# Small products of an RWKV-7 recurrence spread over four array positions instead of two, in a one-core decoder step

## The chip, the cores and the metric

The kernel runs on one core of a Trainium2 chip. A core has a matrix engine (TensorE, "PE" in the profile, its weight loads "PEld"), VectorE ("DVE"), ScalarE ("ACT"), GpSimd ("POOL") and SyncE, whose queue ("SPq") issues the transfers. The metric is the device time of one execution in microseconds (us), median of several runs; lower is better. For a shorter look at one execution there is a profile, with a trace of every instruction.

## The reference

One layer of a decoder trunk on 256 prompt rows and 8 x 4 sample rows, width 2048. A combined input projection feeds two groups of heads, a retention group (8 heads of 256) and an RWKV-7 group (32 heads of 64); one output projection closes the layer. The change lies in the RWKV group:

```
def rwkv7_recurrence(r, w, k, v, kk, a, s0):
    def step(s, inp):
        r_t, w_t, k_t, v_t, kk_t, a_t = inp
        sa = jnp.einsum('bhvk,bhk->bhv', s, -kk_t)
        s = (s * w_t[:, :, None, :] + sa[..., None] * (kk_t * a_t)[:, :, None, :]
             + v_t[..., None] * k_t[:, :, None, :])
        return s, jnp.einsum('bhvk,bhk->bhv', s, r_t)
...
o_rw = group_norm(o_rw, RWKV_GN_EPS) * ln_x_w + ln_x_b
o_rw = o_rw + jnp.sum(r_h * k_h * r_k, axis=-1, keepdims=True) * v_h
y = (jnp.concatenate([y_ret, y_rw], axis=-1) @ w_out)
```

## The kernel before

**Projections.** The inputs `h` and the weights are split into a high and a low fp32r part; each block of weights is loaded (`raw`), split (`whi` by ScalarE, `wlo` by VectorE or GpSimd) and multiplied three times into `acc` (high x high, high x low, low x high). These 128x288 products are most of TensorE's work and the filler between everything else.

**Head pairs.** The RWKV heads are worked in eight rounds q = 0 to 7 of four heads (`rwkv_blocks(q)`); within a round p = 0, 1 are the two tile halves and h (or x) the two heads on partitions 0 to 63 and 64 to 127. The 256 prompt rows are 8 chunks of 32 (`CH`); the sample rows are a ninth "chunk" (c = 8). A tile row of 64 holds two kinds of rows of 32: in `SC` (the masked products), `UV` and `XR` the lower 32 partitions of each head belong to the unknowns of the recurrence, the upper 32 to values and outputs. `quad(h, i)` is quarter i of head h, 32 partitions.

A round goes: `main_gen` makes `AR` and `BK`, multiplies them into `scp` and masks them into `SC`; `turn_gen` turns `BK` into `BKt`, with half of `UV` as scratch; `inv_gen` inverts the 32x32 triangles by a 15-step recurrence on VectorE and two products (`iva`, `ivb`); `main_gen` turns the values into `UV` and multiplies them (`avp`) into `XR`; `chain_gen` walks the eight chunks, three dependent products each (`ch`: XR by WT, UV by BKt, S by AR); `sample_gen` does c = 8; `out_gen` multiplies `SC` by `UV` (`ops`), adds it to `XR`, normalises, turns it back (`on`) and writes `y`.

**What sets the order.** The program is written by one pass in which every generator yields; `tick` steps those whose modelled inputs are ready by a clock of modelled costs, between groups of three projection products. `wait(name)` and `flag(name)` are dependencies between generators at that time, `drain` steps the generators until a flag is set, with no projection product in between. Tiles with one tag share memory, so that a new one must wait for the old one's readers: `UV`, `AR`, `BK`, `XR` have one buffer each. `AR` of round q has tag AR for even q and BK for odd q; in round 7 `BK` takes tag AR. `pch` has two PSUM buffers ("ch") and `ptp` three.

A product of few rows and columns takes only part of the 128x128 array: its input partitions choose rows, its output partitions choose columns. `mm` and `mm4` issue the same matmul; `mm4` only tells the cost model that consecutive products go to four different positions. All matmuls of this group are fp32, and each appears in the trace as two passes, each with its own weight load.

**The end.** The output projection (`out_group`) needs `y` split into `yhi`, `ylo` in the order of `korder`; its first sixteen k tiles lie in `O[0]` to `O[8]`, and `split_gen` does not start on `O[9]` before round 7's `y` is done (flag `("rw", 7)`). In the list of blocks, `od` (nine blocks) stands ahead of the first block that needs `O[9]`, and is itself behind `drain(("ops", 7))`.

Of the kernel before, what the change touches and what calls it, by code (L numbers as in the profile page):

```python
# [10 lines left out]
F32 = mybir.dt.float32  # L11
F32R = mybir.dt.float32r
AF = mybir.ActivationFunctionType
# [88 lines left out]
def tile_hybrid_step(  # L102
# [585 lines left out]
    def rwkv_blocks(q):  # L688
# [95 lines left out]
        def main_gen():  # L784
# [17 lines left out]
            yield  # L802
            yield from wait(("la", q))
            if q > 1:
                yield from wait(("ops", q - 2))
            ar = mx.tile([P, 2, 9, 2, CH], F32, tag="BK" if q % 2 else "AR", name="AR")
            AR = [ar[:, p] for p in range(2)]
            for p in range(2):
# [35 lines left out]
            UV = mx.tile([P, 2, 9, 64], F32, tag="UV", name="UV")  # L844
            B.update(AR=AR, BKt=BKt, SC=SC, UV=UV)
            mk = K("mwkv")
            flat = lambda t: t.rearrange("p a t -> p (a t)")
            yield PART
# [16 lines left out]
            spawn(bonus_gen(kps))  # L865
            vw = B["vw"]
            yield from wait(("turn", q))
            V.transpose(UV[:, 0, :, 32:64], c9(vw[:, 0, :]))
            yield
            for h in range(2):  # L870
# [81 lines left out]
        def inv_gen():  # L952
# [45 lines left out]
            S.copy(itmp[0:32], ps[0:32, 0:256])  # L998
            V.tensor_copy(itmp[64:96], ps[64:96, 0:256])
            yield PART  # L1000
            ps = tps("ivb")
            for i in range(2 * NC):
                for a in ha2:
                    mm(ps[a.start:a.start + HB, HB * i:HB * i + HB], itmp[a, HB * i:HB * i + HB], wv[a, i, HB:])
            for a in ha2:
                a = slice(a.start, a.start + HB)
                V.tensor_copy(wv[a, :, HB:], ps[a, 0:256].rearrange("s (i t) -> s i t", t=HB))
            yield
            flag(("inv", q))

# [120 lines left out]

        def out_gen():
            SC, UV, XR = B["SC"], B["UV"], B["XR"]
            bst = rwp.tile([P, 18, 6], F32, tag="bst", name="bst")
            gst = rwp.tile([P, 3, 18], F32, tag="gst", name="gst")
            yield PART
            ops, op8 = [pch.tile([P, 512], F32, tag="ch", name="ops") for p in range(2)], tps("ops")
# [8 lines left out]
            tt(V, XR[:, :, 8, :], op8[:, 0:128].rearrange("p (a k) -> p a k", a=2), XR[:, :, 8, :], ADD)  # L1146
            yield from pace(SPC)
            flag(("ops", q))
            for p in range(2):
                for c in range(9):  # L1150
                    V.bn_stats(bst[:, 9 * p + c], XR[:, p, c, :])
# [10 lines left out]
            tt(G, var, var, nhalf[:, 0:18], ALU.pow)  # L1162
            yield
            for p in range(2):
                tt(V, XR[:, p], XR[:, p], gst[:, 0, 9 * p:9 * p + 9].unsqueeze(2).to_broadcast([P, 9, 64]), SUB)
                yield
            for p in range(2):
                o = XR[:, p]
                tt(V, o, o, gst[:, 2, 9 * p:9 * p + 9].unsqueeze(2).to_broadcast([P, 9, 64]), MUL)
# [4 lines left out]
                yield  # L1174
                if p == 1:
                    for h in range(2):
                        S.copy(o[quad(h, 1), :, 0:32], o[quad(1 - h, 1), :, 32:64])
                    yield
                V.transpose(c9(on), o[:, :, 32 - 32 * p:64 - 32 * p])
# [438 lines left out]
```

## Time and profile before

| | |
|---|---|
| median of 3 runs | 1561.44 us (1560.08 to 1562.62) |
| the profiled execution's own time | 1563.12 us |
| its span, first to last instruction | 1561.3 us |
| mean granted TensorE clock | 0.973 of full |
| TensorE / VectorE / ScalarE / GpSimd busy | 94% / 75% / 50% / 30% of the span |

A busy TensorE is one with some matmul in flight. All instructions go through one recording helper, so that the source line is always L255, and a group is known by its tiles: `XR<-ops,XR` writes XR from ops and XR. "32*64 32x64 x72" behind a matmul is the weights' shape (input rows by output rows), what it streams, and how many stand in a row.

### The profile page before, as it was taken

How to read it: one execution, taken by the hardware profiler on the slowest of the kernel's cores; microseconds unless marked ns; L12 is line 12 of the kernel's file. 1: busy time of each engine (PE TensorE's matmuls, PEld its weight loads, DVE VectorE, ACT ScalarE, POOL GpSimd, SP SyncE). 2: the span in 40 equal slices, each digit the busy share in tenths (PEclk: the TensorE clock that was granted, in tenths of full speed). 3: DMA queues.
4: the chain of work that ended last, by engine and by line, in shares of the span. 5: the costliest groups of instructions: out<-in, count | busy, mean ns of one | idle time of the engine just before them, and what ended most of it. 6: DMA issues, size and time to landing. Idle time of an engine off the chain costs nothing. (4 is left out here: it accounts for less than half of the span.)

```text
span 1561.3 us, 37454 instructions
## 1 busy us (share of the span) xinstructions
PE 1463.4 (94%) x14194; PEld 1305.5 (84%) x14194; DVE 1165.6 (75%) x2889; ACT 778.4 (50%) x1698; POOL 462.4 (30%) x469
## 2 busy tenths in 40 slices
PE   4889999999999999899999999999999989999996
PEld 1668887888888878888888899879987977999996
DVE  2434787998788878967987799789878987855453
ACT  2224564464445644644555546545653554455443
POOL 0001322442343145323422353245243422202010
PEclk8889999999999999999999999999999999999998
DMA  9996654674476557645764566466536544675553
GB/s 286 341 347 213 196 156 129 183 195 146 126 240 193 146 146 220 189 119 154 216 182 137 154 180 174 114 170 179 155 101 182 159 133 111 193 237 167 158 162 115
DMA packets 347761, 277.30 MB, mean 178 GB/s; under 512 B 90270, under 2 KB 346110, under 8 KB 346868
## 3 DMA queue, kind: packets, MB, share of 16 engines
q1 hardware_dynamic: 347580, 274.91, 60.5%
q8 instruction: 111, 1.82, 0.5%
q14 instruction: 70, 0.57, 0.1%
HBM read 248.80 MB, written 26.03 MB: 176 GB/s over the span
## 5 line engine op out<-in xcount | busy, mean ns | idle before, releaser
L255 PE MATMUL acc<-Hhi,whi 128*128 128x288 f32 (+2 forms) x2080 | 618.6, 312 | 13.3 <-ACT whi L255 5.3
L255 PE MATMUL acc<-Hlo,whi 128*128 128x288 f32 (+2 forms) x2080 | 618.6, 309 | 0.0
L255 ACT CAST whi<-raw 128x512 fp32r<-128x512 f32 (+1 forms) x648 | 395.4, 618 | 353.0 <-PE acc L255 209.2
L255 POOL TENSOR_TENSOR wlo<-raw,whi 128x512 fp32r<-128x512 f32 x224 | 311.0, 1392 | 758.5 <-ACT whi L255 546.0
L255 PE MATMUL acc<-Hhi,wlo 128*128 128x288 f32 (+2 forms) x2080 | 458.5, 302 | 14.8 <-DVE wlo L255 13.9
L255 PEld LDWEIGHTS acc<-Hhi,whi 128*128 128x128 f32 (+1 forms) x2080 | 397.5, 191 | 42.7 <-issue 11.3
L255 PEld LDWEIGHTS acc<-Hlo,whi 128*128 128x128 f32 (+1 forms) x2080 | 398.4, 192 | 17.3 <-issue 8.1
L255 DVE TENSOR_TENSOR wlo<-raw,whi 128x512 fp32r<-128x512 f32 (+1 forms) x424 | 304.8, 724 | 121.7 <-ACT whi L255 117.0
L255 PEld LDWEIGHTS acc<-Hhi,wlo 128*128 128x128 f32 (+1 forms) x2080 | 340.5, 191 | 22.0 <-DVE wlo L255 19.7
L255 PE MATMUL acc<-ylo,whi 128*128 128x288 f32 x480 | 136.4, 298 | 0.7 <-DVE ylo L255 0.7
L255 PE MATMUL acc<-yhi,whi 128*128 128x288 f32 x480 | 135.9, 298 | 1.0 <-ACT whi L255 1.0
L255 PE MATMUL acc<-yhi,wlo 128*128 128x288 f32 x480 | 101.5, 297 | 0.1
L255 PEld LDWEIGHTS acc<-yhi,whi 128*128 128x128 f32 x480 | 90.4, 188 | 1.4 <-ACT whi L255 1.3
L255 PEld LDWEIGHTS acc<-ylo,whi 128*128 128x128 f32 x480 | 90.4, 188 | 1.3 <-DVE ylo L255 1.0
L255 PEld LDWEIGHTS acc<-yhi,wlo 128*128 128x128 f32 x480 | 76.3, 189 | 0.7 <-POOL wlo L255 0.3
L255 PE MATMUL adaps<-raw,cT 128*32 128x256 f32 x768 | 56.3, 409 | 7.8 <-DMA raw<-in_w_ada_dram 7.8
L255 DVE COPY UV<-ch 32x64 f32<-32x64 f32 x128 | 28.9, 225 | 29.1 <-ACT UV L255 26.1
L255 ACT COPY UV<-ch 32x64 f32<-32x64 f32 x128 | 25.5, 199 | 47.8 <-PE ch L255 46.0
L255 DVE SCALAR_TENSOR_TENSOR s0b<-s0b,ups 128x512 f32<-128x512 f32 x64 | 41.0, 681 | 9.0 <-PE ups L255 8.9
L255 PEld LDWEIGHTS adaps<-raw,cT 128*32 128x32 f32 x768 | 20.2, 114 | 30.4 <-DMA raw<-in_w_ada_dram 15.3
L255 POOL TENSOR_TENSOR rot<-rot,rt 128x288 f32<-128x288 f32 x32 | 29.1, 932 | 44.7 <-DVE rt L255 44.7
L255 DVE SCALAR_TENSOR_TENSOR S<-ch,dec,SP 128x64 f32<-128x64 f32 x112 | 30.5, 278 | 13.8 <-PE ch L255 12.7
(260 smaller groups left out, 1966.8 us busy)
## 6 DMA issues: line engine op xcount, KB each, us to landing
raw<-in_w_in_dram SPq DMA_DIRECT2D x512, 256.0 KB, 3.1
raw<-in_w_ada_dram SPq DMA_DIRECT2D x64, 512.0 KB, 8.3
raw<-in_w_out_dram SPq DMA_DIRECT2D x128, 256.0 KB, 3.0
raw<-in_w_ada_dram SPq DMA_DIRECT2D x64, 256.0 KB, 2.8
s0b<-in_state_ret_dram SPq DMA_DIRECT2D x64, 256.0 KB, 4.6
out_dram<-s0b SPq DMA_DIRECT2D x64, 256.0 KB, 3.2
y<-in_x_prompt_dram SPq DMA_DIRECT2D x4, 1024.0 KB, 6.6
s0r<-in_state_rwkv_dram SPq DMA_DIRECT2D x128, 32.0 KB, 2.8
```

The source lines that it names most:

```text
L255: return f(*a, **k)
```

## The change

It touches the four small products that lie at only two array positions at a time, and what reads them.

`avp` (values): the product for an odd chunk goes to the neighbouring 32 columns, so that four consecutive products lie at four positions; 32 output rows each where there were 64, in one PSUM buffer where there were two. ScalarE then writes it to `XR` with two more copies that move the odd chunks' halves to their place.

`ops` (outputs): only the output columns `CH:` of `SC` are multiplied, 32 output rows each, odd chunks again in neighbouring columns. The sum goes to a tile `O` of its own, five chunk slots for each p where there were nine, laid over `AR`'s memory (over `UV`'s in round 6). Group norm then works on 10 columns and 2 x 320 elements instead of 18 and 2 x 576; sixteen short ScalarE copies in place of six longer ones bring it back into `XR` for the transposes.

`iva`, `ivb` (inversion): the second half's products (p = 1) go to the neighbouring columns; the copies out of PSUM are split in two.

Waits: `AR` of round q waits for `("xr", q - 2)`, which `out_gen` sets after its last transpose, where it waited for `("ops", q - 2)`; in round 7 `turn_gen` waits for `("xr", 6)` before it takes `UV`.

```diff
@@ main_gen
-                yield from wait(("ops", q - 2))
+                yield from wait(("xr", q - 2))
...
-            avps, av8 = [pch.tile([P, 512], F32, tag="ch", name="avp") for p in range(2)], tps("avp")
-            for p in range(2):
-                for c in range(9):
-                    for h in hs2:
-                        v = slice(h.start + 32, h.stop)
-                        t = avps[p][h, 64 * c:64 * c + 64] if c < 8 else av8[h, 64 * p:64 * p + 64]
-                        mm(t, SC[v, p, c, :], UV[v, p, c, :])
-            for p in range(2):
-                act(XR[:, p, 0:8, :].rearrange("p c k -> p (c k)"), avps[p], AF.Copy, scale=K("amask"))
+            avp, av8 = pch.tile([P, 512], F32, tag="ch", name="avp"), tps("avp")
+            av5 = avp.rearrange("p (a j k) -> p a j k", a=2, j=4)
+            xr5 = XR[:, :, 0:8, :].rearrange("p a (j b) k -> p a j b k", b=2)
+            for p in range(2):
+                for c in range(8):
+                    for x in range(2):
+                        mm4(av5[quad(x, c % 2), p, c // 2], SC[quad(x, 1), p, c, 0:CH], UV[quad(x, 1), p, c, :])
+            for p in range(2):
+                for x in range(2):
+                    mm(av8[hs2[x], 64 * p:64 * p + 64], SC[quad(x, 1), p, 8, :], UV[quad(x, 1), p, 8, :])
+            for b in (1, 0):
+                act(xr5[:, :, :, b], av5, AF.Copy, scale=K("amask"))
+            for x in range(2):
+                S.copy(xr5[quad(x, 0), :, :, 1], av5[quad(x, 1)])
...
@@ turn_gen
+            if q == 7:
+                yield from wait(("xr", 6))
+            B["UV"] = mx.tile([P, 2, 9, 64], F32, tag="UV", name="UV")
...
@@ inv_gen (ivb in the same way)
-            for i in range(2 * NC):
-                for a in ha2:
-                    mm(ps[a, HB * i:HB * i + HB], SC[a, i // NC, i % NC, 0:CH], MR[a, i, :])
+            for c in range(NC):
+                for p in range(2):
+                    i = NC * p + c
+                    for a in ha2:
+                        mm4(ps[a.start + 32 * p:a.stop + 32 * p, HB * i:HB * i + HB], SC[a, p, c, 0:CH], MR[a, i, :])
...
@@ out_gen
+            O = UV.rearrange("p a c k -> p a (c k)") if q == 6 else B["ar"].rearrange("p a c x t -> p a (c x t)")
+            O = O[:, :, 0:320].rearrange("p a (j k) -> p a j k", j=5)
...
-                    for h in hs2:
-                        t = ops[p][h, 64 * c:64 * c + 64] if c < 8 else op8[h, 64 * p:64 * p + 64]
-                        mm(t, SC[h, p, c, :], UV[h, p, c, :])
-            for p in range(2):
-                xv = XR[:, p, 0:8, :].rearrange("p c k -> p (c k)")
-                tt(V, xv, ops[p], xv, ADD)
...
+                    for x in range(2):
+                        t = op5[quad(x, 1 - c % 2), p, c // 2] if c < 8 else op8[quad(x, 1), 64 * p:64 * p + 64]
+                        mm4(t, SC[hs2[x], p, c, CH:], UV[hs2[x], p, c, :])
+            tt(V, O[:, :, 0:4], op5, xr5[:, :, :, 0], ADD)
+            for x in range(2):
+                tt(V, O[quad(x, 0), :, 0:4], op5[quad(x, 0)], xr5[quad(x, 1), :, :, 1], ADD)
...
                 for h in range(2):
-                    S.copy(o[quad(h, 0), :, 32 - 32 * p:64 - 32 * p], o[quad(h ^ p, 1), :, 0:32])
...
+                    for i in range(2):
+                        for b in range(2):
+                            S.copy(XR[quad(h, i), p, b::2, 0:32], O[quad(h ^ p, 1 - b), p, 0:5 - b, 32 * i:32 * i + 32])
```

The numbers of matmuls are the same in both programs. On TensorE, in round 0, the burst of `avp` between two projection products (an entry here is a matmul, two passes in the trace; 64x64 is the output):

```order
 L255 MATMUL acc<-Hlo,whi 128x288
 L255 MATMUL acc<-Hhi,whi 128x288
-L255 MATMUL avp<-UV,SC 64x64 x36
+L255 MATMUL avp<-UV,SC 32x64 x32
+L255 MATMUL avp<-UV,SC 64x64 x4
 L255 MATMUL acc<-Hlo,whi 128x288
 L255 MATMUL acc<-Hhi,wlo 128x288 x2
```

In round 0 the burst stays where it was, with 32 narrower products and the four of the sample rows unchanged. On VectorE in round 7, `turn_gen`'s first transposes (`UV<-BK`, `BKt<-BK`), before:

```order
L255 TENSOR_TENSOR SC<-scp,cst_85 128x64
L255 TENSOR_TENSOR XR<-XR,gst 128x576
L255 TENSOR_TENSOR wlo<-raw,whi 128x512
L255 STREAM_TRANSPOSE UV<-BK 128x9x32
L255 STREAM_TRANSPOSE BKt<-BK 128x9x32
L255 TENSOR_TENSOR XR<-XR,gst 128x576
```

and after (`on<-XR` is round 6's last transpose, `itmp` and `zt` round 7's inversion):

```order
L255 STREAM_TRANSPOSE on<-XR 128x288
L255 TENSOR_TENSOR itmp<-zt 32x108
L255 TENSOR_TENSOR zt<-zt,itmp 32x2x6x9
L255 TENSOR_TENSOR wlo<-raw,whi 128x512
L255 SCALAR_TENSOR_TENSOR on<-on,pt_88,y 128x288
L255 SCALAR_TENSOR_TENSOR y<-on,pt_88,y 128x288
L255 TENSOR_TENSOR itmp<-zt 32x100
L255 TENSOR_TENSOR zt<-zt,itmp 32x2x5x10
L255 STREAM_TRANSPOSE UV<-BK 128x9x32
L255 STREAM_TRANSPOSE BKt<-BK 128x9x32
```

The turn has moved from among the normalising steps of round 6 to behind round 6's last transpose. On TensorE at the start of the output projection (`ypair`, `yhi`, `ylo` are its right-hand sides), the end of round 7's chain, before:

```order
L255 MATMUL acc<-ypair,whi 128x288 x4
L255 MATMUL acc<-ypair,wlo 128x288 x2
L255 MATMUL ch<-XR,WT 32x64 x4
L255 MATMUL ch<-UV,BKt 64x64 x4
L255 MATMUL acc<-yhi_18369,whi 128x288
```

and after:

```order
L255 MATMUL acc<-ypair,whi 128x288 x4
L255 MATMUL acc<-ypair,wlo 128x288 x2
L255 MATMUL ch<-XR,WT 32x64 x4
L255 MATMUL ch<-UV,BKt 64x64 x4
L255 MATMUL ch<-S_18413,AR 64x64 x2
L255 MATMUL ch<-S_18417,AR 64x64 x2
L255 MATMUL ch<-XR,WT 32x64 x4
L255 MATMUL rcr<-s0b,qp 32x256 x8
L255 MATMUL rcr<-vf,scq 32x256 x4
L255 MATMUL ups<-kv_18312 128x256 x4
L255 MATMUL ch<-UV,BKt 64x64 x4
L255 MATMUL acc<-yhi_18366,whi 128x288
```

More of the chain stands here with no projection product between its steps. Counted in projection products from the program's start, `ops` of round 7 has moved from number 6252 to 6303; the first product that needs `O[9]` is number 6504 in both.

## Rows read from the trace of the kernel before

**Rows 1.** The page: span, and each engine's busy time.

```profile
span 1561.3 us, 37454 instructions
PE 1463.4 (94%) x14194; PEld 1305.5 (84%) x14194; DVE 1165.6 (75%) x2889; ACT 778.4 (50%) x1698; POOL 462.4 (30%) x469
```

**Rows 2.** Stretches: length, busy PE, PEld, DVE, ACT, POOL, clock, DMA, GB/s.

```profile
200.00:1200.00 1000.00, 966.87 (x9855) 857.57 (x9858) 837.75 (x2084) 529.12 (x1135) 361.55 (x343) 0.99 0.58 164
1200.00:1335.00 135.00, 125.40 (x1377) 112.77 (x1378) 110.46 (x282) 69.40 (x149) 41.81 (x44) 0.95 0.49 133
```

**Rows 3.** TensorE's waits from 190 to 1200 us: total, times, longest.

```profile
PE acc L255 <- DVE wlo L255: 11.0, 14, 2.3
...
PE ch L255 <- DVE S L255: 2.8, 6, 1.1
...
PE ch L255 <- DVE XR L255: 1.4, 3, 0.7
```

**Rows 4.** TensorE's timeline, bursts at two positions: start, length, what, passes.

```profile
215.74 2.31 PE L255 MATMUL avp<-UV,SC 32*64 32x64 f32 x72
217.99 0.40 PE L255 MATMUL acc<-Hlo,whi 128*128 128x288 f32 x1
...
227.75 1.19 PE L255 MATMUL iva<-MR,SC 32*32 32x16 f32 x64
...
230.82 0.97 PE L255 MATMUL ivb<-WT,itmp 32*16 32x16 f32 x64
...
259.32 0.41 PE L255 MATMUL ups<-UV,SC 32*32 32x64 f32 x8
...
307.45 2.31 PE L255 MATMUL ops<-UV,SC 64*64 64x64 f32 x72
```

**Rows 5.** The same timeline, bursts at four positions.

```profile
236.10 0.31 PE L255 MATMUL ch<-XR,WT 32*32 32x64 f32 x8
...
238.18 0.35 PE L255 MATMUL ch<-UV,BKt 64*64 64x64 f32 x8
...
1225.20 1.28 PE L255 MATMUL scp<-AR,BK 64*64 64x64 f32 x72
```

**Rows 6.** Groups by shape: count, total busy us, mean ns; idle before, releaser.

```profile
L255 DVE TENSOR_TENSOR XR<-XR,gst 128x576 f32<-128x576 f32 x32 | 26.1, 816 | 0.0
L255 DVE BATCH_NORM_STATS2 bst<-XR 128x6 f32<-128x64 f32 x144 | 19.6, 209 | 0.0
L255 DVE TENSOR_TENSOR XR<-ops,XR 128x512 f32<-128x512 f32 x16 | 11.1, 691 | 11.5 <-PE ops L255 11.5
L255 ACT COPY XR<-XR 32x288 f32<-32x288 f32 x48 | 20.7, 430 | 19.1 <-DVE XR L255 18.5
L255 ACT COPY UV<-ch 32x64 f32<-32x64 f32 x128 | 25.5, 199 | 47.8 <-PE ch L255 46.0
L255 POOL TENSOR_TENSOR gst<-gst,nhalf 128x18 f32<-128x18 f32 x8 | 26.3, 3290 | 0.7
```

**Rows 7.** VectorE's timeline: round 7's first turn, round 6's last transpose.

```profile
1229.13 0.47 DVE L255 STREAM_TRANSPOSE UV<-BK 128x288 f32<-128x288 f32 x1
...
1253.31 0.48 DVE L255 STREAM_TRANSPOSE on<-XR 128x288 f32<-128x288 f32 x1
```

**Rows 8.** TensorE's timeline in round 7, with its waits in brackets.

```profile
1257.40 2.19 PE L255 MATMUL avp<-UV,SC 32*64 32x64 f32 x36 [3.23 <-ACT UV L255]
...
1324.87 0.74 PE L255 MATMUL ch<-UV,BKt 64*64 64x64 f32 x8 [2.92 <-DVE UV L255]
...
1328.32 3.43 PE L255 MATMUL ops<-UV,SC 64*64 64x64 f32 x72
```

**Rows 9.** VectorE's timeline: the low half of `O[9]`.

```profile
1364.91 0.75 DVE L255 TENSOR_TENSOR ylo<-y,yhi 128x576 fp32r<-128x576 f32 x1
```

**Rows 10.** The chain that ended last: retention's `rcr`, a dense run of projection products.

```profile
1331.74 1.43 PE rcr L255 x24
...
1432.84 24.39 PE acc L255 x183
```

More of the change, by code (lines that the diff above doesn't have):

```diff
@@ L804, in main_gen @@
             if q > 1:
-                yield from wait(("ops", q - 2))
+                yield from wait(("xr", q - 2))
             ar = mx.tile([P, 2, 9, 2, CH], F32, tag="BK" if q % 2 else "AR", name="AR")
             AR = [ar[:, p] for p in range(2)]
+            B["ar"] = ar
             for p in range(2):
@@ L843, in main_gen @@
             SC = mx.tile([P, 2, 9, 64], F32, tag="SC", name="SC")
-            UV = mx.tile([P, 2, 9, 64], F32, tag="UV", name="UV")
-            B.update(AR=AR, BKt=BKt, SC=SC, UV=UV)
+            B.update(AR=AR, BKt=BKt, SC=SC)
             mk = K("mwkv")
@@ L867, in main_gen @@
             yield from wait(("turn", q))
+            UV = B["UV"]
             V.transpose(UV[:, 0, :, 32:64], c9(vw[:, 0, :]))
@@ L994, in inv_gen @@
             ps = tps("iva")
-            for i in range(2 * NC):
-                for a in ha2:
-                    mm(ps[a, HB * i:HB * i + HB], SC[a, i // NC, i % NC, 0:CH], MR[a, i, :])
-            S.copy(itmp[0:32], ps[0:32, 0:256])
-            V.tensor_copy(itmp[64:96], ps[64:96, 0:256])
+            for c in range(NC):
[4 more added lines that the diff above has]
+            for p in range(2):
+                s = slice(128 * p, 128 * p + 128)
+                S.copy(itmp[0:32, s], ps[32 * p:32 * p + 32, s])
+                V.tensor_copy(itmp[64:96, s], ps[64 + 32 * p:96 + 32 * p, s])
             yield PART
             ps = tps("ivb")
-            for i in range(2 * NC):
-                for a in ha2:
-                    mm(ps[a.start:a.start + HB, HB * i:HB * i + HB], itmp[a, HB * i:HB * i + HB], wv[a, i, HB:])
+            for c in range(NC):
+                for p in range(2):
+                    i = NC * p + c
+                    for a in ha2:
+                        mm4(ps[a.start + 32 * p:a.start + 32 * p + HB, HB * i:HB * i + HB], itmp[a, HB * i:HB * i + HB],
+                            wv[a, i, HB:])
             for a in ha2:
-                a = slice(a.start, a.start + HB)
-                V.tensor_copy(wv[a, :, HB:], ps[a, 0:256].rearrange("s (i t) -> s i t", t=HB))
+                for p in range(2):
+                    o = a.start + 32 * p
+                    V.tensor_copy(wv[a.start:a.start + HB, NC * p:NC * p + NC, HB:],
+                                  ps[o:o + HB, 128 * p:128 * p + 128].rearrange("s (i t) -> s i t", t=HB))
             yield
@@ L1133, in out_gen @@
             SC, UV, XR = B["SC"], B["UV"], B["XR"]
-            bst = rwp.tile([P, 18, 6], F32, tag="bst", name="bst")
-            gst = rwp.tile([P, 3, 18], F32, tag="gst", name="gst")
+            O = UV.rearrange("p a c k -> p a (c k)") if q == 6 else B["ar"].rearrange("p a c x t -> p a (c x t)")
+            O = O[:, :, 0:320].rearrange("p a (j k) -> p a j k", j=5)
+            bst = rwp.tile([P, 10, 6], F32, tag="bst", name="bst")
+            gst = rwp.tile([P, 3, 10], F32, tag="gst", name="gst")
             yield PART
-            ops, op8 = [pch.tile([P, 512], F32, tag="ch", name="ops") for p in range(2)], tps("ops")
+            ops, op8 = pch.tile([P, 512], F32, tag="ch", name="ops"), tps("ops")
+            op5 = ops.rearrange("p (a j k) -> p a j k", a=2, j=4)
+            xr5 = XR[:, :, 0:8, :].rearrange("p a (j b) k -> p a j b k", b=2)
             for p in range(2):
                 for c in range(9):
-                    for h in hs2:
-                        t = ops[p][h, 64 * c:64 * c + 64] if c < 8 else op8[h, 64 * p:64 * p + 64]
-                        mm(t, SC[h, p, c, :], UV[h, p, c, :])
-            for p in range(2):
-                xv = XR[:, p, 0:8, :].rearrange("p c k -> p (c k)")
-                tt(V, xv, ops[p], xv, ADD)
-            tt(V, XR[:, :, 8, :], op8[:, 0:128].rearrange("p (a k) -> p a k", a=2), XR[:, :, 8, :], ADD)
+                    for x in range(2):
[4 more added lines that the diff above has]
+                tt(V, O[quad(x, 0), :, 0:4], op5[quad(x, 0)], xr5[quad(x, 1), :, :, 1], ADD)
+                tt(V, O[quad(x, 1), :, 4], op8[quad(x, 1), 0:128].rearrange("p (a k) -> p a k", a=2), XR[quad(x, 1), :, 8], ADD)
             yield from pace(SPC)
@@ L1149, in out_gen @@
             for p in range(2):
-                for c in range(9):
-                    V.bn_stats(bst[:, 9 * p + c], XR[:, p, c, :])
+                for j in range(5):
+                    V.bn_stats(bst[:, 5 * p + j], O[:, p, j])
                 yield
@@ L1161, in out_gen @@
             ts(G, var, var, 1.0 / 64, 64e-5, MUL, ADD)
-            tt(G, var, var, nhalf[:, 0:18], ALU.pow)
+            tt(G, var, var, nhalf[:, 0:10], ALU.pow)
             yield
             for p in range(2):
-                tt(V, XR[:, p], XR[:, p], gst[:, 0, 9 * p:9 * p + 9].unsqueeze(2).to_broadcast([P, 9, 64]), SUB)
+                tt(V, O[:, p], O[:, p], gst[:, 0, 5 * p:5 * p + 5].unsqueeze(2).to_broadcast([P, 5, 64]), SUB)
                 yield
             for p in range(2):
-                o = XR[:, p]
-                tt(V, o, o, gst[:, 2, 9 * p:9 * p + 9].unsqueeze(2).to_broadcast([P, 9, 64]), MUL)
+                tt(V, O[:, p], O[:, p], gst[:, 2, 5 * p:5 * p + 5].unsqueeze(2).to_broadcast([P, 5, 64]), MUL)
                 on = rwp.tile([P, NR], F32, tag="on", name="on")
@@ L1172, in out_gen @@
                 for h in range(2):
-                    S.copy(o[quad(h, 0), :, 32 - 32 * p:64 - 32 * p], o[quad(h ^ p, 1), :, 0:32])
[L1174 to L1177, printed above, removed]
+                    for i in range(2):
+                        for b in range(2):
+                            S.copy(XR[quad(h, i), p, b::2, 0:32], O[quad(h ^ p, 1 - b), p, 0:5 - b, 32 * i:32 * i + 32])
                     yield
-                V.transpose(c9(on), o[:, :, 32 - 32 * p:64 - 32 * p])
+                V.transpose(c9(on), XR[:, p, :, 0:32])
                 yield
```

## The prediction

> **What bounds the kernel now.** The page comes first [rows 1]: TensorE has a matmul in flight for 1463.4 of 1561.3 us, VectorE is busy for 75%. An average over a kernel with a start and an end hides who is short where, so the stretches come next [rows 2]. From 200 to 1200 us, most of rounds 0 to 6, TensorE is busy for 966.87 of 1000 us at 0.99 of its clock and VectorE for 837.75; at the end of round 7 (1200 to 1335 us) TensorE stands idle for 9.6 of 135 us and its clock is at 0.95. The waits say who ends the 33 us of idleness in the long stretch [rows 3]: the largest item is `wlo` from VectorE, 11.0 us in 14 waits of at most 2.3 us. So in rounds 0 to 6 time taken off TensorE is time off the kernel, as long as VectorE, 16% free, keeps up; in round 7 the order of the dependent steps counts too.
>
> **TensorE's bursts.** The timeline shows what each burst costs [rows 4]. `avp` starts at 215.74 and the next projection product at 217.99: 2.25 us, 0.06 less than the length in its row, since a matmul's end overlaps the next one's start. The offset is about the same for every burst, so I take differences of lengths. `ops` is as long, 2.31; `iva` 1.19; `ivb` 0.97. Rounds 0 to 6 repeat these lengths.
>
> What is a pass worth at two positions and at four? Three pairs of rows tell it [rows 4, 5]. (a) 64-wide products at four positions: `scp`, 72 passes, 1.28 us; `ch<-UV,BKt`, 8 passes, 0.35; so (1.28 - 0.35) / 64 = 14.5 ns a pass. (b) 32x32 weights streaming 64: `ups` at two positions, 8 passes, 0.41; `ch<-XR,WT` at four, 8 passes, 0.31. If the pace doubles with the positions, 8 passes differ by 8 times the four-position pace, which is then 0.10 / 8 = 12.5 ns, and what is left, 0.41 - 8 x 0.025 = 0.21 us, is a burst's fixed part. (c) `avp` and `ops` themselves, 64 wide at two positions: (2.31 - 0.21) / 72 = 29.2 ns, twice the 14.5 of (a). So doubling the positions halves the pace, and `scp` shows it over 72 passes of the very pattern that is now used.
>
> The new `avp` is 64 passes of kind (b) at four positions and 8 of kind (c): 0.21 + 64 x 0.0125 + 8 x 0.0292 = 1.24 us, 1.07 less. The new `ops` is 72 of kind (b): 0.21 + 72 x 0.0125 = 1.11 us, 1.20 less (its weights have 64 input rows where (b) has 32, which makes no difference between `avp` and `ops` today). Dear bound, the 14.5 ns of (a): 0.94 and 1.06. Cheap bound, the lowest pace of any row, `ivb`'s (0.97 - 0.21) / 64 = 11.9 ns: 1.11 and 1.24.
>
> `iva` and `ivb` already run at 15.3 and 11.9 ns. No row goes below 11.9, so whether TensorE can start passes faster is not shown. From below: no gain. From above: half of each pace, 0.49 and 0.38 us. I take 0.35 for `iva` (halfway between falling to 11.9, which is 0.22, and halving) and 0.19 for `ivb`, halfway.
>
> A round: 1.07 + 1.20 + 0.35 + 0.19 = 2.81 us; eight rounds 22.5 us, between 8 x 2.00 = 16 and 8 x 3.22 = 25.8.
>
> **The other engines.** VectorE per round [rows 6]. Adding `ops` took two of 0.69 and one of about 0.28; it now takes one of 0.69, two of 512 elements on 32 partitions (0.69 each, if partitions don't count) and two short ones, 0.97 more. Statistics: eight fewer at 19.6 / 144 = 0.136, 1.09 less. The four normalising steps go from 576 to 320 elements: 0.82 by the row, some of it waiting; by 0.69 for 512 I put the gain at 0.27 each, 1.1 less. The copies after `iva` and `ivb` become six shorter ones for three, about 0.4 more. Net 0.8 less, 6.5 us in the kernel. GpSimd's power goes from 18 to 10 columns: 3.29 x 8 / 18 = 1.5 us sooner. ScalarE gets more: two copies of 512 elements after `avp` (1.4), and sixteen copies of 128 or 160 elements, between the 199 ns of 64 and the 430 ns of 288, say 0.28, for six of 0.43: 1.9. With `iva`, 3.4 a round, 27 us on 778.4, covered by ScalarE's idle half. None of this is on TensorE's path unless `whi`, `wlo` or a chain step comes later for it. VectorE's load over the long stretch stays near 833, in about 982 us instead of 1000: its free share falls from 16 to 15%, and the 33 us of waits should grow by a tenth at most. I give 2 us back, between 0 and 6.
>
> **Waits.** `AR` of round q waits for round q - 2's `xr` instead of its `ops`: a whole round lies between, nothing is lost. In round 7 it is different. `turn_gen` now waits for round 6's last transpose: 1229.13 and 1253.31 today, 24.2 us apart [rows 7]. Behind it stand `BKt`'s eight ScalarE copies, the values' transposes, `avp`, then the chain, `ops`, the normalising and the last seven splits of the output projection. The inversion has been a parallel branch that ended later, so only a part shows: counted in the order, `ops` comes 51 projection products later, at 24.39 / 183 = 0.133 us [rows 10] 6.8 us. During those 6.8 us TensorE does other work, which is then missing in two places.
>
> First, at the start of the output projection, three more chain steps (S by AR, XR by WT, UV by BKt) stand with no projection product between them; the last is covered by retention products. Such steps cost 0.47 (2.8 / 6) to 1.1 us and 0.47 to 0.7 us where TensorE waits for S and XR today [rows 3]: 0.9 to 1.8, I take 1.5. In that place TensorE already waits 2.92 us, after which `ops` ran 3.43 us instead of 2.31, at the lower of its two clock levels (1.2 against 2.4 GHz) [rows 4, 8]; 0.5 us for a little longer at that level.
>
> Second, before the first product that needs `O[9]`. Today `ops` starts at 1328.32 and `ylo` of `O[9]` ends at 1365.66, 37.3 us later [rows 8, 9]. Less 2.3 for the faster burst, 1.5 for the power, 1.1 for statistics and 1.1 for normalising, plus 1.0 for the adds and 1.8 for ScalarE's copies in line: about 34 us. The cover: 201 products (6504 - 6303) at 0.133 = 26.8; the burst itself 1.1; of retention's products 16 passes of `rcr` at 1.43 / 24 [rows 10], 1.0, and four shorter bursts at an estimated 0.65: 31.5. So TensorE waits about 2.5 us there, where today 252 x 0.133 = 33.6, the burst's 3.4 and retention's products more than cover the 37.3. Bounds 0 and 6.
>
> `avp` itself waits 3.23 us today for `UV` [rows 8]; it now stands behind `iva` with more projection products ahead of it. That wait may go or grow: 0, between -4 and +4. Round 7 in all: 4.5 us lost, between -2 and 12.
>
> **The sum.** -22.5 + 2 + 4.5 = -16 us. On the profiled execution's 1563.1 us (span 1561.3 and 1.8 around it) that is 1547.1. The median of the runs is 1.7 below that execution, so 1545.4, say 1545.5.
>
> **The rivals.**
>
> 1. *Neighbouring columns don't run at once.* Four positions on the same two sets of rows would then be worth no more than two, and only the narrower weights would help: `ups`'s two-position pace of 25 ns gives `avp` 0.21 + 64 x 0.025 + 0.23 = 2.04 and `ops` 2.01, 0.57 a round, 4.6 us; less 6.5 given back: about 1563, no change. Against it: `scp` and `ch` reuse the same two sets of rows on other columns, and (a) is half of (c). The Trainium skill (TensorE: Matmul & The Clock Gate, Part 3, "The mechanism") says that a weight load overlaps matmuls in flight only where their row groups differ, which would make this rival the forecast; the rows of `scp` disagree. 4%.
>
> 2. *VectorE sets the pace.* If the freed time turns into waits for `wlo` and chain steps, what remains is VectorE's own 6.5 us, less round 7's 4.5: about 1559.5, no change to speak of. For it: VectorE at 84%, and `wlo` the first of the waits. Against it: these are 11 us in 1000. 8%.
>
> 3. *Slower: round 7's turn goes in full.* If the 24.2 us by which the turn moves stood idle on TensorE, 22.5 - 2 would be gone: 1561.4 + 3.7 = 1565. It decides from 20.5 us of idleness in round 7. For it: one chain without branches from the turn to `O[9]`. Against it: the order moves `ops` by 6.8 us only, because the inversion was the longer branch. 5%.
>
> **How the numbers follow.** The forecast has 83%; its own spread (16 to 25.8 for the bursts, 0 to 6, -2 to 12) runs from 1534 to 1563 with all ends together, which is unlikely, and from 1537 to 1554 with most of it. Rivals 1 and 2 lie between 1559 and 1563. The range from 1537 to 1556 leaves out the rivals and a few per cent at the low end. A measurement of this kernel tells 0.2%, 3 us, from no change: faster 0.87, same 0.08, slower 0.05.
>
> **What would show it.** `avp` near 1.24 and `ops` near 1.11 us; `iva` and `ivb` at or under 0.97; the long stretch shorter by 2 to 3 us a round; in round 7, waits at the chain's end and before `O[9]` of 2 to 6 us together beyond today's. Wrong if `avp` and `ops` stay above 1.9 us, if `wlo` waits grow by more than 6 us, or if round 7 loses more than 12.

## The result and the profile after

The changed kernel takes 1572.9 us (median of 8 runs, 1568.1 to 1583.0) against 1562.0 for the kernel before: 1.0077 of its time, 95% interval 1.0050 to 1.0104. It was forecast at 1545.5 (1537 to 1556) and faster; it is slower by 11 us. The profiled execution took 1572.1 us.

The page, span and busy time of each engine, answers to [rows 1]:

```profile
span 1570.3 us, 37553 instructions
PE 1454.3 (93%) x14194; PEld 1287.3 (82%) x14194; DVE 1165.8 (74%) x2871; ACT 805.1 (51%) x1802; POOL 445.4 (28%) x463
```

The stretches of [rows 2], in the same columns:

```profile
200.00:1200.00 1000.00, 951.48 (x9803) 839.17 (x9804) 836.97 (x2072) 548.22 (x1210) 338.83 (x331) 0.98 0.58 163
1200.00:1335.00 135.00, 123.78 (x1311) 110.02 (x1313) 111.20 (x271) 72.98 (x163) 48.69 (x51) 0.94 0.53 145
```

TensorE is busy for 951 of the long stretch's 1000 us where it was busy for 967, and not because the kernel is through with them sooner. VectorE's busy time did not fall, ScalarE has 19 us more in this stretch and 27 in the whole.

The bursts on TensorE's timeline, as in [rows 4] (start, length, what, passes):

```profile
219.53 1.47 PE L255 MATMUL avp<-UV,SC 32*32 32x64 f32 x72
...
230.69 0.73 PE L255 MATMUL iva<-MR,SC 32*32 32x16 f32 x64
...
317.01 1.31 PE L255 MATMUL ops<-UV,SC 64*32 64x64 f32 x72
...
700.21 0.69 PE L255 MATMUL ivb<-WT,itmp 32*16 32x16 f32 x64
...
1346.46 1.31 PE L255 MATMUL ops<-UV,SC 64*32 64x64 f32 x72
```

`avp` fell from 2.31 to 1.47, `ops` from 2.31 to 1.31 (in round 7 from 3.43), `iva` from 1.19 to 0.73, and `ivb` from 0.97 to 0.69 in four of the eight rounds; in the other four it took 0.99 to 1.33. So TensorE has what the change was to bring. What it waits for, from 190 to 1200 us as in [rows 3] (total, times, longest):

```profile
PE acc L255 <- DVE wlo L255: 10.5, 12, 2.5
PE acc L255 <- ACT rot L255: 8.4, 5, 4.6
PE acc L255 <- DVE vw L255: 5.7, 3, 3.3
PE acc L255 <- ACT whi L255: 5.3, 6, 1.5
...
PE adaps L255 <- DVE rot L255: 3.3, 1, 3.3
PE acc L255 <- POOL wlo L255: 2.8, 5, 0.7
```

In the kernel before, the same view had:

```profile
PE acc L255 <- ACT rot L255: 4.5, 4, 2.9
...
PE acc L255 <- DVE vw L255: 2.7, 2, 2.1
...
PE acc L255 <- ACT whi L255: 0.6, 2, 0.4
PE acc L255 <- POOL wlo L255: 0.5, 1, 0.5
```

No single wait explains the loss; splits and evacuations (the steps that take a finished block out of PSUM, as those for `rot` and `vw` do), which ScalarE and VectorE do, are late by a little in many places. And a wait costs more than its length. Stretches of 5 us around two of them, in the columns of [rows 2]:

```profile
455.00:460.00 5.00, 2.70 (x15) 1.90 (x16) 4.84 (x22) 0.00 (x0) 3.23 (x1) 0.58 0.22 58
460.00:465.00 5.00, 5.00 (x29) 4.69 (x29) 2.20 (x11) 1.24 (x2) 3.14 (x5) 0.74 0.92 301
640.00:645.00 5.00, 4.00 (x17) 4.04 (x18) 3.56 (x11) 1.24 (x2) 0.00 (x0) 0.51 0.77 177
645.00:650.00 5.00, 5.00 (x94) 4.68 (x94) 2.91 (x8) 0.73 (x2) 0.00 (x0) 0.81 0.65 150
```

The 3.3 us wait for VectorE's `rot` ends in the first pair, at 457.30, the 3.3 us wait for `vw` in the second, at 641.00. The granted clock falls shortly before the wait ends (to 0.51 in one slice, which is the lower level, 1.2 GHz) and comes back only within the next slice. The table of such slices from 200 to 1400 us has 7 dips before and 12 after; each of them begins during a wait of TensorE or behind one or two, of 1.6 to 4.6 us together.

All TensorE rows of the two timelines, added up: for each row, the time from its start to the next row's start without the wait in brackets, by kind, and the waits apart (us):

| | the four bursts | waits | projection products | everything else |
|---|---|---|---|---|
| before | 55.8 | 83.7 | 1136.8 | 272.6 |
| after | 33.8 | 101.0 | 1141.2 | 281.7 |
| difference | -22.0 | +17.3 | +4.4 | +9.1 |

The last two columns are the same instructions in both kernels. Of their 13.5 us the granted clock in the same rows accounts for 11.0 (each row's time multiplied by what its clock lacks of the full one); the other 2.5 stay unexplained. The bursts' gain is there, -22.0, and 2.5 of it is clock as well, since some bursts of the kernel before ran at the lower level and none does now. Waits and slower rows take 30.8. That makes +8.8 of the 9.0 us between the two spans.

### The profile page after: what moved, and what is told of

Read it like the earlier page. It is cut to its first block, busy times and chain, and to the rows that moved or that the text cites. A ratio compares the mean times of both kernels' runs of the same rounds, so it can differ in the third digit from the quotient of the medians.

```text
span 1570.3 us, 37553 instructions
## 1 busy us (share of the span) xinstructions
PE 1454.3 (93%) x14194; PEld 1287.3 (82%) x14194; DVE 1165.8 (74%) x2871; ACT 805.1 (51%) x1802; POOL 445.4 (28%) x463
## 5 line engine op out<-in xcount | busy, mean ns | idle before, releaser
L255 POOL TENSOR_TENSOR wlo<-raw,whi 128x512 fp32r<-128x512 f32 x218 | 298.4, 1373 | 742.2 <-ACT whi L255 532.9
L255 DVE TENSOR_TENSOR wlo<-raw,whi 128x512 fp32r<-128x512 f32 (+1 forms) x430 | 315.2, 738 | 139.0 <-ACT whi L255 133.2
L255 PE MATMUL adaps<-raw,cT 128*32 128x256 f32 x768 | 60.4, 429 | 12.3 <-DMA raw<-in_w_ada_dram 9.0
L255 DVE SCALAR_TENSOR_TENSOR s0b<-s0b,ups 128x512 f32<-128x512 f32 x64 | 41.0, 682 | 15.1 <-PE ups L255 14.5
L255 ACT COPY XR<-AR 32x160 f32<-32x160 f32 x112 | 34.7, 310 | 15.1 <-DVE AR L255 13.7
```

The costliest lines, as they stand in the source:

```text
L255: return f(*a, **k)
```

## The experiments

Four theories. A: the change's additional ScalarE copies hold up splits and evacuations. B: the builder's new order is to blame. C: round 7's later turn. D, from the second series on: TensorE's freed time only turns into waits for steps that last as long as before, and into lower clock.

All were timed beside the kernel before; ratios are to its time in the same series. Medians, and in the last two columns means over a kernel's timed executions, uncertain by some 1 us, at most 2: with T the span and c the mean granted clock, T x (1 - c) is about what the lower clock costs (its level is half, and TensorE is nearly always busy), and T x c is the rest.

| kernel | us | ratio, 95% interval | T x c | T x (1 - c) |
|---|---|---|---|---|
| before | 1562 to 1564.5 | 1 | 1517.0 | 45.2 |
| after | 1572.9 | 1.0077 (1.0050 to 1.0104) | 1519.0 | 53.1 |
| p_inv | 1559.4 | 0.9980 (0.9966 to 0.9993) | 1515.7 | 42.3 |
| p_avp | 1564.6 | 1.0006 (0.9988 to 1.0024) | 1516.2 | 46.5 |
| p_out | 1564.2 | 1.0007 (0.9993 to 1.0021) | 1517.8 | 44.6 |
| p_cost | 1561.4 | 0.9984 (0.9970 to 0.9999) | 1519.8 | 39.5 |
| x_oldplan_new | 1573.9 | 1.0069 (1.0044 to 1.0094) | 1519.0 | 53.0 |
| x_newplan_old | 1575.7 | 1.0079 (1.0058 to 1.0101) | 1524.7 | 49.4 |
| n_new_mm | 1566.8 | 1.0012 (0.9995 to 1.0030) | 1515.1 | 49.7 |
| s_short | 1563.8 | 1.0002 (0.9990 to 1.0013) | 1517.0 | 45.0 |
| s_copies | 1570.2 | 1.0038 (1.0021 to 1.0054) | 1520.4 | 48.5 |
| s_vlight | 1555.6 | 0.9951 (0.9934 to 0.9969) | 1510.0 | 44.3 |
| s_short_vlight | 1557.8 | 0.9957 (0.9943 to 0.9971) | 1510.2 | 45.1 |
| s_half | 1563.9 | 1.0001 (0.9986 to 1.0016) | 1511.0 | 50.9 |
| s_half_vlight | 1554.3 | 0.9945 (0.9931 to 0.9959) | 1502.8 | 49.7 |
| x_oldplan_avpinv | 1566.7 | 1.0024 (1.0013 to 1.0035) | 1515.6 | 49.5 |
| g_sub | 1566.6 | 1.0016 (1.0005 to 1.0027) | 1520.5 | 43.9 |
| n_nocopy | 1564.8 | 1.0001 (0.9986 to 1.0015) | 1510.4 | 52.2 |
| n_poolcopy | 1579.9 | 1.0091 (1.0071 to 1.0111) | 1518.5 | 59.7 |
| x_oldplan_inv | 1563.5 | 0.9991 (0.9978 to 1.0004) | 1518.1 | 43.7 |

**The parts alone.** Each takes one part of the diff: p_inv `iva` and `ivb`, p_avp `avp`, p_out `ops` and `out_gen` with its waits. p_cost takes the kernel before and only calls the four products by the other name (here `avp`):

```diff
-                        mm(t, SC[v, p, c, :], UV[v, p, c, :])
+                        mm4(t, SC[v, p, c, :], UV[v, p, c, :])
...
```

> The change of iva and ivb alone. Its bursts get 0.46 and 0.28 us shorter a round as in the changed kernel (6 us in eight rounds), and ScalarE and VectorE get four short copies more. Theory A (ScalarE's many short copies in out_gen hold up the evacuations and splits that TensorE waits for): the gain arrives nearly in full, about 1556 us. Theory B (the builder puts all the work into another order, and the new order happens to make TensorE wait more): anything from 1550 to 1572, with waits before projection products that have nothing to do with the inversion. Theory C (round 7's later turn costs it): 1556.

> The change of avp alone: its burst 0.84 us shorter a round (6.7 us), two more ScalarE copies of 512 elements a round. Theory A: about 1556 to 1558 us. Theory B: anything from 1550 to 1572. Theory C: 1555.

> The change of ops and out_gen alone, with the wait of round 7's turn: its burst 1.0 us shorter a round (8 us), sixteen short ScalarE copies for six longer ones, VectorE's normalising shorter. Theory A: nearly all of the loss is here, 1568 to 1574 us, with longer waits for rot, whi, vw. Theory B: anything from 1550 to 1575, and the three parts' differences to the kernel before don't add up to the whole change's +11. Theory C: about +5 in round 7 and the gain of 8 before it, 1559.

> The kernel before with its own instructions, in which avp, ops, iva and ivb are only told to the builder's cost model as four-position bursts, so that it takes them for shorter than they are and orders everything anew. No burst gets shorter and no copy is added. Theories A and C: 1562 us, within 3. Theory B: a difference of 4 to 12 us either way from the order alone.

None of the parts brings what its bursts save, and none brings the loss: -0.2%, +0.06%, +0.07% do not add up to +0.77%. p_cost, with no instruction changed, moved by -0.16%. But each of these kernels is also put into an order of its own, so that they can't tell instructions from order. p_cost hardly tests the order either: its trace has TensorE's other products in the order of the kernel before for the first 8851 of 12018 passes, up to 1134 us; the changed kernel leaves that order after 1575.

**Instructions and order apart.** x_oldplan_new writes the new instructions while the builder is charged the old ones' costs, x_newplan_old the reverse. Both forms of each piece stand in the program; one runs for the cost account alone, the other is issued without being accounted:

```diff
+    def both(old, new, em=None, pl=None):
+        em, pl = em or EMIT, pl or PLAN
...
+        emit[0] = False
+        (old if pl == "old" else new)()
+        emit[0], mute[0] = True, True
+        (old if em == "old" else new)()
+        mute[0] = False
...
-                yield from wait(("xr", q - 2))
+                yield from wait(("xr" if PLAN == "new" else "ops", q - 2))
...
+            both(avp_old, avp_new)
```

Every other instruction then stands, on every engine, where it stands in the kernel whose order is copied. In x_oldplan_new `out_gen` of round 6 stays old, so that round 7's turn has nothing to wait for. n_new_mm is the changed kernel with `mm` for `mm4` in its four bursts, a third order.

> The new bursts, copies and normalising in the order of the kernel before: the builder is charged the old instructions' costs while it writes the new instructions, so that every other instruction stands where it stood (out_gen of round 6 stays old, so that round 7's turn needs no wait). Theory A (the copies and evacuations of the change cost more than its bursts save): still about 1568 to 1574 us. Theory B (the new order is to blame): the bursts' gain of 17 us shows, 1543 to 1550. If the freed time only becomes waiting for VectorE (rival 2): about 1558 to 1562.

> The other way round: the old bursts, copies and normalising in the order of the changed kernel, its waits included. Theory A: 1562 us or a little more for round 7's turn, up to 1566. Theory B: the order alone costs the gain and more, so without the shorter bursts 1575 to 1592.

> The changed kernel's instructions, with its four bursts told to the cost model as two-position ones, which gives a third order. Theory A: 1568 to 1576 us, like the changed kernel. Theory B: some other time between 1545 and 1575, with nothing to tie it to the changed kernel's 1573.

Each of the two is enough for the loss. The new instructions in the old order lose 0.69%: 15.5 us shorter bursts, and yet slower. The old instructions in the new order lose 0.79%. Together they lose 0.77%, not the sum: in the new order the new instructions are no worse than the old. A third order of the same new instructions is at +0.12%. Theory C is out as the main cause: x_oldplan_new has no later turn and loses 0.69%. Where the new order loses is read from x_newplan_old's TensorE waits, 190 to 1200 us:

```profile
PE acc L273 <- DVE wlo L273: 11.6, 12, 2.5
PE acc L273 <- ACT rot L273: 6.1, 5, 4.2
PE acc L273 <- ACT whi L273: 5.9, 7, 1.5
```

Most of the changed kernel's longer `whi` and `rot` waits are here, with the old instructions: they belong to the order for the greater part. The new instructions in the old order (x_oldplan_new) have 3.0 us for `whi` and 5.0 for `rot`.

**Shorter bursts and nothing else.** From here on every kernel stands in the order of the one before. s_short tries to shorten `avp` and `ops` without touching another engine: one product of 512 columns with the first chunk's weights for the eight of 64. s_copies adds ScalarE copies and shortens nothing. s_vlight leaves out four VectorE steps of `out_gen`, s_short_vlight does both.

```diff
-                for c in range(9):
-                    for h in hs2:
...
-                        mm(t, SC[v, p, c, :], UV[v, p, c, :])
+                    for h in hs2:
...
+                        mm(avps[p][h, :], SC[v, p, 0, :], UV[v, p, 0:8, :].rearrange("p c k -> p (c k)"))
```

> The kernel before, in its own order and with every copy and VectorE step of it, with only the bursts of avp and ops made short: each (p, head) is one product of 512 columns with the first chunk's weights instead of eight of 64 (seven of eight chunks get wrong weights). About 1.2 us less TensorE time a burst, 19 us in eight rounds; no other engine's work changes. Theory A (the change's additional copies eat the gain): the gain shows in full, 1543 to 1548 us. Theory D (between its bursts TensorE is held up by steps that last as long as before, so that time taken off it turns into waits, and waits lower its clock): 1558 to 1566, with 15 to 20 us more of waits.

> The kernel before, in its own order, with ten further ScalarE copies a round (avp's two written twice, and eight copies of 160 elements ahead of out_gen's transposes, except in round 6), about 3.7 us of ScalarE a round as in the changed kernel; no burst is shorter. Theory A: 1570 to 1580 us. Theory D: the copies lie beside other work, 1562 to 1567.

> The kernel before, in its own order, with four VectorE steps of each out_gen left out (the subtraction of the mean, twice 576 elements, and the step with the weight and the bonus, twice 288): about 2.2 us of VectorE a round, 18 us in the kernel. Theory A: 1560 to 1563 us. Theory D with VectorE as what holds up TensorE: 1548 to 1556.

> Both together: short bursts and the lighter VectorE. Theory A: 1543 to 1547 us. Theory D: the two gains need each other, so clearly below either alone, 1540 to 1550.

s_short missed: its timeline shows bursts of eight passes of 512 columns and eight of 64 (the sample rows; the view names the first shape alone), 4608 columns as in the 72 short ones, and they last nearly as long. So its time, and that of s_short_vlight beside s_vlight, tells nothing of shorter bursts.

```profile
310.23 2.21 PE L273 MATMUL ops<-UV,SC 64*64 64x512 f32 x16
```

s_vlight is 0.49% faster, 8 us for 17 us of VectorE's busy time (1148.9 for 1165.6); s_copies is 0.38% slower, 6 us for 24 us of ScalarE's (802.8 for 778.4). Work on those two engines is worth time, in part.

s_half does what s_short was to do: it multiplies p = 0 alone and lets the readers of p = 1 read the same PSUM tile.

```diff
-                for c in range(9):
+                    for c in range(8 * p, 9):
...
-                act(XR[:, p, 0:8, :].rearrange("p c k -> p (c k)"), avps[p], AF.Copy, scale=K("amask"))
+                    act(XR[:, p, 0:8, :].rearrange("p c k -> p (c k)"), avp, AF.Copy, scale=K("amask"))
```

> The kernel before in its own order, with avp and ops multiplied for p = 0 alone (and the sample rows); what was read from the second half's PSUM tile is read from the first one's, so p = 1's prompt products are left out. 40 passes instead of 72: each burst about 1.0 us shorter, 16 us in eight rounds; every copy and VectorE step stays as long as it was. Theory A (time off the bursts is time off the kernel, and the change's additional work eats it): 1546 to 1551 us. Theory D (the freed time turns into waits for other engines and lower clock): 1558 to 1564.

> The same with the four VectorE steps of out_gen left out as well (no subtraction of the mean, no weight and bonus). s_vlight alone was 8 us faster than the kernel before. Theory A: another 2 to 8 us below s_half, 1540 to 1546. Theory D with VectorE in the way: the burst's gain shows once VectorE is lighter, so clearly below s_vlight's 1555.6, at 1540 to 1548; if it stays at 1553 to 1557, the bursts are worth nothing even so.

Its timeline shows that this time the bursts are short, 1.38 us for 2.31:

```profile
217.43 1.38 PE L273 MATMUL avp<-UV,SC 32*64 32x64 f32 x40
...
308.24 1.38 PE L273 MATMUL ops<-UV,SC 64*64 64x64 f32 x40
```

Added up as above, the bursts take 41.3 us instead of 55.8. The time is 1.0001. So 14.5 us less TensorE work, no other engine changed, the same order, and nothing gained in the median (the interval leaves room for 2 us). Over its executions T x c falls by 6.0 us and T x (1 - c) rises by 5.7: 8.5 of the 14.5 don't show even at full clock, and the lower clock takes the other 6. That the 8.5 are waits is read from the one profiled execution, whose waits, counted at full clock, are 5.9 us longer than before. This execution was a quick one: its span is 7.0 us shorter, so that single executions do keep some of the gain. With VectorE made lighter (s_half_vlight against s_vlight) it is much the same: 7.2 less at full clock, 5.4 more at the lower one.

**Which work brings the loss.** x_oldplan_avpinv issues the new `avp`, `iva` and `ivb` with the old `out_gen`. g_sub gives `out_gen`'s subtraction of the mean to GpSimd in the kernel before.

> The order of the kernel before with the new avp, iva and ivb (bursts about 11 us shorter, two more 512-element ScalarE copies and three more short ones a round) and the old out_gen. The whole change in this order was 1.0069 of the kernel before. If out_gen's work brings the loss: 1550 to 1560 us. If avp's additional copies do: 1566 to 1572. Theory D alone, without either: 1560 to 1565.

> The kernel before in its own order, all its work done, with the subtraction of the mean in out_gen (twice 576 elements a round) given from VectorE to GpSimd in rounds 0 to 6: 1.4 us of VectorE a round less, 2 to 3 us of GpSimd more. If VectorE's load is what holds TensorE up (s_vlight): 1556 to 1560 us. If GpSimd then delays the wlo splits that it takes: 1562 to 1568. Theory A: 1562.

x_oldplan_avpinv loses 0.24%, about a third of x_oldplan_new's 0.69%; the larger part, by difference, is `out_gen`'s. g_sub is slower by 0.16%: GpSimd is no free place either.

n_nocopy is x_oldplan_new without the sixteen short copies, n_poolcopy has them on GpSimd in rounds 0 to 5; x_oldplan_inv is the inversion's part in the old order. The line taken out is that of n_nocopy, the last one stands in its place in n_poolcopy.

```diff
-                            S.copy(XR[quad(h, i), p, b::2, 0:32], O[quad(h ^ p, 1 - b), p, 0:5 - b, 32 * i:32 * i + 32])
+                            pass
...
+                            S.copy(dst, src) if q == 7 else G.tensor_copy(dst, src)
```

> The new instructions in the old order (x_oldplan_new, 1.0069 of the kernel before) without the sixteen short ScalarE copies a round that bring the outputs back into XR (left out in rounds 0 to 5 and 7, so the transposes read unfinished values): 16 x 0.31 = 5 us of ScalarE a round less. If these copies bring out_gen's share of the loss: 1560 to 1566 us. If VectorE's sums and avp's copies do: 1569 to 1574.

> The new instructions in the old order, all work done, with those sixteen copies on GpSimd in rounds 0 to 5 (ScalarE in round 7). If ScalarE's place in the way is the cause: 1562 to 1568 us. If GpSimd, which also takes wlo splits, is then late: 1570 to 1580.

> The order of the kernel before with the new iva and ivb alone: 0.74 us less a burst pair, 6 us in eight rounds, and three more short copies a round. p_inv, the same edit with an order of its own, was 0.998 of the kernel before. If time off the bursts is worth nothing: 1562 to 1565 us, and p_inv's gain was its order's. If it is worth its size: 1556 to 1559.

Without the sixteen copies the loss is gone: 1.0001. This doesn't price the change's additional copying alone: the copies left out take 34.7 us of ScalarE, while the kernel before spends 18.1 us in the same rounds on its six longer ones, so that n_nocopy asks less of ScalarE than the kernel before (769.3 us busy against 778.4). The sixteen copies are worth 0.68%; how much of that their excess over the six costs was not run. n_nocopy also has 15.8 us shorter bursts and is no faster than the kernel before. On GpSimd the copies cost more still. x_oldplan_inv is within the noise of no change, so nothing shows that p_inv's 0.2% is the inversion's own; p_inv and p_cost (0.9984, by order alone) are the only versions here, of those that do all the work, that beat both kernels, and by little.

A way from the copies to TensorE shows in VectorE's waits from 190 to 1345 us: total, times, longest. The kernel before:

```profile
DVE wlo L255 <- ACT whi L255: 31.1, 32, 3.3
```

The new instructions in the same order, with the copies (x_oldplan_new):

```profile
DVE wlo L273 <- ACT whi L273: 38.0, 41, 5.1
...
DVE on L273 <- ACT XR L273: 3.1, 4, 1.1
```

and without them (n_nocopy):

```profile
DVE wlo L273 <- ACT whi L273: 33.5, 36, 3.8
```

In all three traces ScalarE's other 1618 instructions stand in the same order: `whi` stands behind the copies, VectorE waits for `whi` to make `wlo`, and waits for the copies themselves ahead of its transposes (`on<-XR`). That what stands behind those on VectorE is then late for TensorE is argued. In the changed kernel the first of these waits is 44.7 us, but that is the order's doing: x_newplan_old, with the old instructions and no additional copy, has as much.

```profile
DVE wlo L273 <- ACT whi L273: 45.2, 37, 4.7
```

## Why the prediction was wrong

**The bursts: right.** -22.5 forecast, -22.0 measured. The pieces were off in opposite ways: `avp` saved 0.84 instead of 1.07 and `ops` 1.00 instead of 1.20, `iva` 0.46 instead of 0.35 and `ivb` 0.28 instead of 0.19, though `ivb` took 0.99 to 1.33 us in four of the eight rounds and saved 0.35 us in all. That the sum comes out so close is in part luck: 2.5 us of it are the bursts that the kernel before ran at the lower clock, which the forecast of 22.5 did not count; at full clock the bursts saved 19.4. Rival 1 is out: `avp` and `ops` do run at four positions on two sets of rows, `ops` at (1.31 - 0.21) / 72 = 15.3 ns a pass where `ups` had 25. The rule of the Trainium skill named with it (TensorE: Matmul & The Clock Gate, Part 3, "The mechanism") does not agree with these rows.

**The other engines: the step that failed.** "I give 2 us back, between 0 and 6" measured 30.8 less round 7's share. It rests on two sentences. "So in rounds 0 to 6 time taken off TensorE is time off the kernel, as long as VectorE, 16% free, keeps up" is refuted by s_half: 14.5 us off TensorE alone brought nothing in the median. 967 busy us of 1000 said that TensorE was seldom idle, not that the rest would be ready sooner if it asked sooner. "The 33 us of waits should grow by a tenth at most": they grew to 48.5. And outside round 7 the prediction gave the clock no term, though [rows 8] had shown one burst at the lower level behind a wait; a wait's second price was left out, 11.0 us on the instructions that did not change. "Covered by ScalarE's idle half" is refuted by s_copies: the amount was right (27 us forecast, 26.7 measured), but 24 us of copies alone cost 6. None of the three signs of being wrong came: `wlo` waits on VectorE went from 11.0 to 10.5 us, and the loss stood in waits for `rot`, `vw` and `whi` instead.

**VectorE.** Forecast 6.5 us lighter; the busy time, in which overlapping instructions count once, is 0.2 heavier. By lengths added up, the change's own steps got 12.8 us shorter: the sums dearer by 7.8 and the copies after the inversion by 3.8, about as forecast, the statistics with their small sums 17.3 cheaper and the normalising 7.1. But `wlo` took 10.6 more. Some of the changed kernel's groups by shape (count, total, mean ns):

```profile
L255 DVE TENSOR_TENSOR AR<-AR,gst 128x320 f32<-128x320 f32 x28 | 16.5, 594 | 0.0
L255 DVE BATCH_NORM_STATS2 bst<-AR 128x6 f32<-128x64 f32 x70 | 10.1, 211 | 0.0
L255 DVE TENSOR_TENSOR AR<-ops,XR 32x512 f32<-32x512 f32 x14 | 9.6, 685 | 0.3
...
L255 ACT COPY XR<-AR 32x160 f32<-32x160 f32 x56 | 18.1, 323 | 14.5 <-DVE AR L255 13.7
L255 ACT COPY XR<-AR 32x128 f32<-32x128 f32 x56 | 16.6, 296 | 0.7
...
L255 DVE TENSOR_TENSOR wlo<-raw,whi 128x512 fp32r<-128x512 f32 x422 | 311.0, 742 | 129.1 <-ACT whi L255 123.2 <-PE acc L255 2.5 <-issue 0.3
```

and the `wlo` splits of the kernel before:

```profile
L255 DVE TENSOR_TENSOR wlo<-raw,whi 128x512 fp32r<-128x512 f32 x416 | 300.6, 727 | 111.9 <-ACT whi L255 107.1 <-PE acc L255 1.3
```

A sum on 32 partitions takes as long as one on 128 (685 ns against 691 in [rows 6]), as assumed. What was not foreseen is that the new order gives VectorE six `wlo` splits that GpSimd had (224 of its splits before, 218 after), at 0.74 us each, and that the others take 15 ns more each; why they do is open.

**Round 7: about right.** 4.5 us forecast. TensorE's timeline there, waits in brackets:

```profile
1330.33 0.74 PE L255 MATMUL ch<-UV,BKt 64*64 64x64 f32 x8 [3.29 <-DVE UV L255]
```

At the chain's end this wait is 3.29 us where it was 2.92, and two steps behind it wait 0.35 and 0.34: 1.1 us for the 1.5 forecast. From `ops` to the low half of `O[9]` it takes 33.3 us, forecast 34, and ahead of the products that need it TensorE waits 1.21 us for `yhi` and 0.59 for `ylo`: 1.8 for the 2.5. The 3.23 us wait ahead of `avp` is gone, and three of 1.65 to 2.03 us for `wlo` and `whi` have come in other places. The sum tests less than the pieces do: counted by projection products, the changed kernel is 7.5 us behind at number 5800 (1228 us before), 4.6 at 6000 and 8.9 from 6700 on, so that round 7 lost 1.4 to 4.3 us by where it is taken to begin. Rival 3, which needed 20.5 us there, is out.

**The order.** The prediction looked for what the new order does in round 7 only. Before it the lag had already grown to 21.6 us (product 2747) and fallen to 4.6 by 6000. The order alone, with the old instructions, costs 12 us (x_newplan_old). That rival was not on the list. Rival 2, at 8%, was nearest to what happened: the freed time did turn into waits, though little of it for `wlo` on VectorE. s_vlight bears out a part of it (8 us for 17); its 1559.5 lacked the clock, the copies and the order.

**What stays open.** Why one order is worth 7 us more than another (n_new_mm against the changed kernel) was not pursued to single waits. That s_half's clock falls over its executions follows from the table; that its longer waits cause it is argued from the slices above, since its one profiled execution happened to be a quick one (clock 0.973, span 1554.3), with the clock of the kernel before. The new order and the new instructions were each shown to be enough for the loss; how they overlap in the changed kernel was not taken apart. Within the instructions, the copies are the likely cause, but the excess of the sixteen over the six was not run by itself.

## What to carry to other kernels

A busy share of 97% did not make TensorE the bound here; shorten the burst alone in an unchanged order first (leaving out half the products will do), and see whether the time moves. Where the order comes from modelled costs, freeze it before judging a part: here the order alone was worth as much as the whole change. And copies on an engine that also feeds the busiest one can cost time however idle it is on average: here 24 us of them, on an engine busy for half the span, cost 6.

## What was unexpected of the hardware

- Long passes gained next to nothing over short ones: eight passes of 512 columns and eight of 64 took 2.21 us, 72 passes of 64 columns 2.31, both 4608 columns at two positions.
- In the records of round 0's `avp`, two passes started together every 58 ns before the change, and four every 56 ns after it.
- The lowest pace of a row before, 11.9 ns a pass, was no floor: `iva` at four positions took 0.73 us for 64 passes, which is (0.73 - 0.21) / 64 = 8.1 ns with the same fixed part taken off.
- GpSimd's power took 1.998 us for 10 columns and 3.29 for 18: 0.16 us a column and some 0.4 fixed.
- Around a wait of 3.3 us TensorE's clock went to the lower of its two levels, and stayed there after the wait: the two slices around the end of the wait for `rot` lost (1 - 0.58) x 5 + (1 - 0.74) x 5 = 3.4 us of full clock, of which some 0.8 fell in the wait itself, where TensorE stood idle anyway.
